# The input projection of a gated ConvFFN by seven products of quarter blocks in place of eight

## The chip, the cores and the metric

The kernel runs on one core of one Trainium2 chip, in one launch. The metric is the device time of a run in microseconds (us), lower is better. The engines are named as the profile names them: PE is TensorE's matmul and PEld its weight load, DVE is VectorE, ACT is ScalarE, POOL is GpSimd, SP is SyncE, whose queue issues nearly all transfers.

## The reference

A trunk of two layers works on 1024 tokens of 1024 features in float32. Each layer adds three branches to the residual stream x: token mixing by four groups of heads, cross-attention to 256 memory tokens, and a gated feed-forward network with a convolution over three tokens. The last one is what matters here:

```python
def conv_ffn(xn, w_in, conv_w, conv_b, w_out):
    h = xn @ w_in
    gate, up = h[..., :D_FF], h[..., D_FF:]
    gp = jnp.pad(gate, ((0, 0), (1, 1), (0, 0)))
    gconv = gp[:, :-2] * conv_w[0] + gp[:, 1:-1] * conv_w[1] + gp[:, 2:] * conv_w[2] + conv_b
    return (jax.nn.silu(gconv) * up) @ w_out

x = x + conv_ffn(rms_norm(x, norm_ffn[l]), w_ffn_in[l], ffn_conv[l], ffn_conv_b[l], w_ffn_out[l])
```

D_FF is 2816, so `w_in` is 1024 x 5632 and `w_out` 2816 x 1024.

## The kernel before

**Layout.** Features lie on partitions and tokens along the free axis: a tile is [128, 1024], 128 features of all tokens. x is 8 such tiles and lives in DRAM (`XD`). A matmul multiplies a block of weights [128 features in, 128 features out] with a tile's tokens, 512 columns at a time, one PSUM bank each.

**Pairs.** Every operand of a large product is split into `hi` (a cast to float32r, on ScalarE) and `lo` (the remainder, a subtraction on VectorE). A product takes three passes, hi hi, hi lo and lo hi (`dense_steps`, lines 344 to 348). `weights` (line 309) loads a block of 512 KB into a "raw" buffer (two of them) and makes its pair in the buffers "whi" and "wlo" (two of each).

**Pools.** Tag "h" has 16 tiles of [128, 1024], tag "t" 16 (work tiles), tag "z" 4 (side tiles), tag "s" 6 small tiles of 512 columns; PSUM has "sc" (two of two banks), "tp" (three banks) and "fl" (one).

**The ffn.** `run` (line 1551) ends the cross-attention with a residual product: `residual` (line 1253) goes over the eight output tiles m, loads x, multiplies, adds from PSUM (line 1260), stores x, and calls `done`. Here that is `finish_x` (line 369): it makes the pair of x times the norm's gain, and adds its squares to the sum in `RB` by ScalarE and GpSimd (line 235). `stats_end` (line 237) turns the sums into the norm's factor per token, spread over partitions in `RB`, with small matmuls (lines 245 and 254). So the ffn's inputs H are 8 pairs in 16 "h" tiles, not yet scaled by the norm's factor; that is put on the products.

The 22 tiles of inner features are made by `ffn_tile` (line 1524), eight, eight and six of them, and after each group the residual product over the group's pairs follows (eight tiles m, weights `w_ffn_out`). A tile multiplies H with the gate's weights and with up's weights: 2 blocks x 8 k x 3 passes x 2 token halves. VectorE takes the gate from PSUM with the norm's factor (line 1531), ScalarE and VectorE make the convolution (lines 1532 to 1539), ScalarE Silu (line 1540), VectorE takes up (line 1543), GpSimd multiplies (line 1544), and the pair of the output goes to two "t" tiles (lines 1546 and 1547).

**Order.** Each engine works through its own queue in order. The order in each queue is set when the kernel is built, by a scheduler that goes by priority (program order) and a timeline; a tile's buffer is reused when the last reader of its former owner is done, and buffers of one tag are handed out in program order. SP's queue holds the transfers of all of these in one line.

Of the kernel before, what the change touches and what calls it, by code (L numbers as in the profile page):

```python
# [30 lines left out]
# columns of the per-layer parameter block  # L31
# [8 lines left out]
# columns of the constants  # L40
# [3 lines left out]
# bands of 128 columns that spread compact rows over partitions  # L44
# [4 lines left out]
class Net:  # L49
# [69 lines left out]
    # --------------------------------------- work that runs in between other work  # L119
    def fill(self, gen, which=0):  # L120
        """Queues a generator that yields the time of what it has emitted."""
        self.queues[which].append(gen)
        return gen

    def pump(self, us, which=0):
        """Emits queued work of about us."""
# [23 lines left out]
    # ---------------------------------------------------------------- set-up  # L150
    def setup(self):
# [37 lines left out]
        self.OD = self.dram([KT, P, S], F32, "od")  # L189

# [3 lines left out]
    # -------------------------------------------------------- reciprocal roots  # L194
    def rsqrt(self, v, out, n):
        """out = 1 / sqrt(v) on [128, n]: bits halved, a Newton step, a step of third order."""
# [17 lines left out]
    # ------------------------------------------------------------ model norms  # L214
    def split_scaled(self, x, g, hi, lo, lo_engine=None):
        """hi + lo = x * g, each of them exact in float32r."""
# [9 lines left out]
    def stats_add(self, st, x, sq=None):  # L226
        """Adds x * x of one tile of features."""
# [9 lines left out]
    def stats_end(self, st, RB, bank=None):  # L237
        """r token-major [128, n / 128], spread over partitions into RB [128, n], and 1 / r^2."""
# [22 lines left out]
    # --------------------------------------------- norms over groups of features  # L261
    def group_sums(self, ps, G, g0, sq, ind, nt=8):
        """Sums of squares per token (partitions) and group: ps[:, t, g0:...]."""
# [7 lines left out]
    def group_rsqrt(self, ps, G, dim, inv, nt=8, times=1.0):  # L271
        """[128, nt * G] of times * r / sqrt(r^2 * mean + eps), of a stream that r still has to scale; inv = 1 / r^2."""
# [14 lines left out]
    def group_spread(self, y, G, band, banks, use, nt=8, rows=None):  # L287
        """Spreads the groups over partitions: use(slice, PSUM) for each half of the tokens.

        Rows over tokens as a float32r pair, g and 32 + g, which a band of ones adds up."""  # L290
# [17 lines left out]
    # ------------------------------------------------------------ dense layers  # L308
    def weights(self, src, K=KT, M=P, lo_engine=None, pool=None):
        """A [128, K, M] block of weights as a float32r pair."""  # L310
# [1341 lines left out]
def _tiles(w):  # L1652
    """[K, 128 n] as n blocks [128, K / 128, 128]."""
    k, n = w.shape
    return w.reshape(k // P, P, n // P, P).transpose(2, 1, 0, 3)
# [79 lines left out]
```

## Time and profile before

| | |
|---|---|
| median of three runs | 3649.74 us (3646.77 to 3653.95) |
| the profiled execution | span of 3645.1 us, 43780 instructions |
| granted TensorE clock, mean | 0.950 |
| busy: PE, DVE, ACT, POOL | 93%, 48%, 35%, 25% of the span |
| ffn of layer 0, with the last residual of cross-attention behind it | about 1117 to 1831 us |
| ffn of layer 1 | about 2930 to 3645 us |

The profile is of one execution. Busy time is the time in which an engine executes; the duration of a matmul holds its way through the pipeline, so several overlap, and the distance from one start to the next is what it costs. Durations of VectorE and GpSimd hold what they wait for inside the instruction. "<-" behind an idle time names what ended it. L12 is line 12 of the kernel.

### The profile page before, as it was taken

What the parts mean: (1) busy time and instruction counts of PE and PEld (TensorE: products, weight loads), DVE (VectorE), ACT (ScalarE), POOL (GpSimd) and SP (SyncE); (2) the same over time, 40 slices, a digit from 0 to 9 for tenths busy, and PEclk for the clock granted to TensorE, in tenths of its full rate; (3) what the DMA queues carried; (4) which work ended last, traced back from release to release, by engine and by line L of the source; (5) the groups of instructions that cost most, each with busy time, mean ns of one, the idle gap of its engine ahead of it and who ended that gap; (6) DMA issues with size and microseconds to landing.
All of it is one profiled execution on the core that took longest, in us unless ns stands there. A gap on an engine that the chain in (4) does not pass through costs nothing. (4 is left out here: it accounts for less than half of the span.)

```text
span 3645.1 us, 43780 instructions
## 1 busy us (share of the span) xinstructions
PE 3407.1 (93%) x17372; PEld 2871.1 (79%) x17372; DVE 1749.7 (48%) x2588; ACT 1271.0 (35%) x2011; POOL 922.3 (25%) x577
## 2 busy tenths in 40 slices
PE   7899778999999999999998988789899999999999
PEld 7777567887778888888897767679777888888887
DVE  4554547875443423423436536669735344234232
ACT  4322446753432212212333225567535222122121
POOL 2221335752111101101113214357422111011010
PEclk9998689999999999999999987889999999999999
DMA  5333234413242131231343332354223411312313
GB/s 162 97 110 98 82 90 137 170 69 138 70 139 76 48 131 58 64 122 53 109 135 100 110 118 82 96 167 137 91 86 106 137 53 58 133 47 74 117 45 123
DMA packets 142624, 367.85 MB, mean 101 GB/s; under 512 B 29842, under 2 KB 46996, under 8 KB 142420
## 3 DMA queue, kind: packets, MB, share of 16 engines
q1 hardware_dynamic: 142196, 364.53, 30.8%
q8 instruction: 137, 2.24, 0.3%
q0 software_dynamic: 224, 0.52, 0.0%
q14 instruction: 67, 0.55, 0.0%
HBM read 252.81 MB, written 104.86 MB: 98 GB/s over the span
## 5 line engine op out<-in xcount | busy, mean ns | idle before, releaser
L319 ACT CAST whi<-raw 128x1024 fp32r<-128x1024 f32 (+2 forms) x262 | 258.4, 986 | 1156.2 <-PE sc L346 728.4
L348 PE MATMUL sc<-h,wlo 128*128 128x512 f32 x1568 | 504.1, 402 | 14.2 <-DVE wlo L320 14.2
L344 PE MATMUL sc<-h,whi 128*128 128x512 f32 x1568 | 504.1, 402 | 9.5 <-ACT h L714 5.3
L346 PE MATMUL sc<-h,whi 128*128 128x512 f32 x1568 | 502.0, 400 | 0.0
L1544 POOL TENSOR_TENSOR z<-z,z 128x1024 f32<-128x1024 f32 x44 | 143.2, 3254 | 1165.0 <-DVE z L1543 1015.2
L348 PEld LDWEIGHTS sc<-h,wlo 128*128 128x128 f32 x1568 | 301.8, 194 | 81.9 <-DVE wlo L320 16.3
L344 PEld LDWEIGHTS sc<-h,whi 128*128 128x128 f32 x1568 | 300.5, 194 | 77.9 <-ACT h L714 6.6
L346 PEld LDWEIGHTS sc<-h,whi 128*128 128x128 f32 x1568 | 301.8, 193 | 66.7 <-issue 2.7
L320 DVE TENSOR_TENSOR wlo<-raw,whi 128x1024 fp32r<-128x1024 f32 (+2 forms) x210 | 255.4, 1216 | 91.4 <-ACT whi L319 91.2
L1260 DVE TENSOR_TENSOR z<-sc,z 128x1024 f32<-128x1024 f32 x64 | 78.4, 1225 | 413.6 <-PE sc L348 413.6
L348 PE MATMUL sc<-t,wlo 128*128 128x512 f32 x896 | 276.4, 389 | 0.1
L346 PE MATMUL sc<-t,whi 128*128 128x512 f32 x896 | 276.2, 389 | 0.0
L344 PE MATMUL sc<-t,whi 128*128 128x512 f32 x896 | 275.7, 389 | 0.4 <-ACT whi L319 0.3
L467 DVE TENSOR_REDUCE smax<-sc 128x1 f32<-128x1024 f32 x192 | 233.6, 1217 | 75.6 <-PE sc L676 56.0
L470 ACT ACTIVATE h<-sc,smax 128x1024 f32<-128x1024 f32 x192 | 214.8, 1121 | 101.5 <-DVE smax L467 76.5
L530 DVE TENSOR_TENSOR s<-tp,s 128x512 fp32r<-128x512 f32 x256 | 173.1, 683 | 100.0 <-ACT s L529 98.2
L344 PE MATMUL fl<-h,whi 128*128 128x512 f32 (+1 forms) x480 | 177.0, 369 | 38.4 <-ACT z L1304 38.4
L348 PEld LDWEIGHTS sc<-t,wlo 128*128 128x128 f32 x896 | 168.0, 188 | 35.8 <-DVE wlo L320 1.0
L344 PEld LDWEIGHTS sc<-t,whi 128*128 128x128 f32 x896 | 168.0, 188 | 35.6 <-ACT whi L319 0.9
L235 POOL TENSOR_TENSOR rb<-rb,z 128x1024 f32<-128x1024 f32 x42 | 114.0, 2713 | 324.2 <-ACT z L234 315.9
L346 PEld LDWEIGHTS sc<-t,whi 128*128 128x128 f32 x896 | 168.2, 188 | 34.9
L525 PE MATMUL tp<-identr,h 128*128 128x128 f32 x1024 | 178.8, 281 | 12.0 <-DVE s L530 8.1
(378 smaller groups left out, 6905.8 us busy)
## 6 DMA issues: line engine op xcount, KB each, us to landing
raw<-w_ffn_in SPq DMA_DIRECT2D x88, 512.0 KB
xd<-z SPq DMA_DIRECT2D x72, 512.0 KB
z<-xd SPq DMA_DIRECT2D x72, 512.0 KB
raw<-w_ffn_out SPq DMA_DIRECT2D x32, 512.0 KB
raw<-w_fm SPq DMA_DIRECT2D x30, 512.0 KB
z<-xT SPq DMA_DIRECT2D x16, 512.0 KB
raw<-w_ck SPq DMA_DIRECT2D x16, 512.0 KB
raw<-w_cv SPq DMA_DIRECT2D x16, 512.0 KB
```

What stands on the lines that cost most here:

```text
L235: nc.gpsimd.tensor_tensor(out=st["acc"], in0=st["acc"], in1=sq, op=ALU.add)
L319: nc.scalar.copy(hi, raw)
L320: (lo_engine or nc.vector).tensor_tensor(out=lo, in0=raw, in1=hi.bitcast(F32), op=ALU.subtract)
L344: nc.tensor.matmul(o, lhsT=hi[:, k, :], rhs=xh[:, f : f + m], start=first, stop=False)
L346: nc.tensor.matmul(o, lhsT=hi[:, k, :], rhs=xl[:, f : f + m], start=False, stop=False)
L348: nc.tensor.matmul(o, lhsT=lo[:, k, :], rhs=xh[:, f : f + m], start=False, stop=last)
L467: nc.vector.tensor_reduce(out=m, in_=sc, axis=AX.X, op=ALU.max, negate=True)
L470: nc.scalar.activation(e, sc, AF.Exp, bias=m, scale=1.0, accum_out=s)
L525: nc.tensor.transpose(tp[:, (2 * j + i) * P : (2 * j + i + 1) * P], w[:, (k + j) * P : (k + j + 1) * P], self.ident)
L530: nc.vector.tensor_tensor(out=el, in0=tp, in1=eh.bitcast(F32), op=ALU.subtract)
L1260: nc.vector.tensor_tensor(out=x, in0=ps, in1=x, op=ALU.add)
L1544: nc.gpsimd.tensor_tensor(out=c, in0=c, in1=g, op=ALU.mult)
```

## The change

The product [gate; up] = W^T H of one tile is seen as a product of 2 x 2 blocks: gate and up are the two rows of blocks, the two halves of the 1024 input features are the inner blocks, the two halves of the tokens are the columns. The form of Winograd and Strassen makes it of seven products of quarter blocks (`PRODUCTS`), each over 4 k and 512 tokens, with sums ahead of and behind them.

- The sums of token blocks are made once in a layer. `ffn_operands` takes the place of `finish_x`: x times the gain is kept whole, and for each of the four k, tile m = k and tile m = k + 4 give seven operands (`quarter_sums`, four sums, two on each of VectorE and GpSimd), each as a pair in one [128, 1024] tile. The residual goes over m in the order 0, 4, 1, 5, 2, 6, 3, 7. For m = 3 and 7 x is scaled in place. 28 tiles of "h" and "t" hold them.
- The sums of weight blocks are made in every tile, four on GpSimd from the two raw blocks, and seven pairs of half size go to the buffers "whi" and "wlo" in turn.
- Products follow one another in three PSUM banks X, Z and Y; X gathers four of them and is read in between; gate and up are put together in SBUF by three copies and three additions, then scaled by `RB`.
- The tile's output goes to DRAM (`GD`). All 22 tiles are made first. Then the three residual products follow, whose operands `load_pair` reads back through a side tile.

Everything else is the same; comments and docstrings are removed.

```diff
         self.OD = self.dram([KT, P, S], F32, "od")
+        self.GD = self.dram([FT, P, S], F32, "gd")
...
-    def residual(self, wsrc, K, H, xsrc, xdst, done=None, alloc=None):
-        nc = self.nc
-        for m in range(KT):
+    def residual(self, wsrc, K, H, xsrc, xdst, done=None, alloc=None, order=range(KT)):
+        nc = self.nc
+        for m in order:
             x = (alloc or self.z_)()
             nc.sync.dma_start(out=x, in_=xsrc[m])
             ps = self.dense_full(self.weights(wsrc(m), K=K), H)
...
-    def ffn_tile(self, l, f, H, alloc):
+    def half_pair(self, x, g, b, lo_engine=None):
+        nc = self.nc
+        hi, lo = b[:, :HF], b[:, HF:]
+        if g is None:
+            nc.scalar.copy(hi, x)
+            (lo_engine or nc.vector).tensor_tensor(out=lo, in0=x, in1=hi.bitcast(F32), op=ALU.subtract)
+        else:
+            self.split_scaled(x, g, hi, lo)
+        return hi, lo
+    def quarter_sums(self, a, b):
+        nc = self.nc
+        tt = nc.gpsimd.tensor_tensor
+        a1, a2, b1, b2 = a[:, :HF], a[:, HF:], b[:, :HF], b[:, HF:]
+        t1, t2, t3, t4 = (self.s_() for _ in range(4))
+        nc.vector.tensor_tensor(out=t1, in0=a2, in1=a1, op=ALU.subtract)
+        nc.vector.tensor_tensor(out=t3, in0=b2, in1=a2, op=ALU.subtract)
+        tt(out=t2, in0=b2, in1=t1, op=ALU.subtract)
+        tt(out=t4, in0=b1, in1=t2, op=ALU.subtract)
+        return {"11": a1, "21": b1, "t2": t2, "t1": t1, "t3": t3, "22": b2, "t4": t4}
+    def ffn_operands(self, l, B):
+        nc = self.nc
+        seen, late = {}, []
+        st = self.stats_begin()
+        def done(m, x):
+            k = m % 4
+            self.stats_add(st, x, self.t_() if k == 3 else None)
+            y = x if k == 3 else self.t_()
+            nc.scalar.activation(y, x, AF.Identity, bias=0.0, scale=self.col(l, C_FFN + m))
+            seen[m] = y
+            if m < 4:
+                return
+            a, b = seen.pop(k), seen.pop(m)
+            if k < 2:
+                for n, v in self.quarter_sums(a, b).items():
+                    B[n].append(self.half_pair(v, None, (self.tr_ if n == "11" else self.h_)()))
+            else:
+                late.append((a, b))
+        def end():
+            sums = [self.quarter_sums(a, b) for a, b in late[:1]]
+            for n in self.PRODUCTS:
+                for i in range(2):
+                    if i == len(sums):
+                        sums.append(self.quarter_sums(*late[1]))
+                    B[n].append(self.half_pair(sums[i][n], None, (self.h_ if n in ("22", "t4") else self.tr_)()))
+        return st, done, end
+    PRODUCTS = ("11", "21", "t2", "t1", "t3", "22", "t4")
+    def ffn_in_tile(self, l, f, B, dst):
         nc, d = self.nc, self.d
-        gp = self.sc_()
-        self.dense(self.weights(d["w_ffn_in"][l, f, 0]), H, [gp[:, :HF], gp[:, HF:]])
-        up = [self.fl_(), self.pv_()]
-        self.dense(self.weights(d["w_ffn_in"][l, f, 1]), H, up)
-        g, c = self.z_(), self.z_()
-        nc.vector.tensor_tensor(out=g, in0=gp, in1=self.RB, op=ALU.mult)
+        raw = []
+        for i in range(2):
+            r = self.tile(self.pw, [P, S], F32, "raw", bufs=2)
+            nc.sync.dma_start(out=r.rearrange("p (k m) -> p k m", m=P), in_=d["w_ffn_in"][l, f, i])
+            raw.append(r)
+        a11, a12, a21, a22 = (r[:, h * HF : (h + 1) * HF] for r in raw for h in range(2))
+        s1, s2, s3, s4 = (self.s_() for _ in range(4))
+        tt = nc.gpsimd.tensor_tensor
+        tt(out=s1, in0=a21, in1=a22, op=ALU.add)
+        tt(out=s2, in0=s1, in1=a11, op=ALU.subtract)
+        tt(out=s3, in0=a11, in1=a21, op=ALU.subtract)
+        tt(out=s4, in0=a12, in1=s2, op=ALU.subtract)
+        A = {"11": a11, "21": a12, "t2": s2, "t1": s1, "t3": s3, "22": s4, "t4": a22}
+        pair = {}
+        for i, n in enumerate(self.PRODUCTS):
+            pair[n] = self.half_pair(A[n], None, self.tile(self.pw, [P, S], F32R, ("whi", "wlo")[i % 2], bufs=2))
+        xz = self.sc_()
+        X, Z, Y = xz[:, :HF], xz[:, HF:], self.pv_()
+        def product(n, ps, first):
+            hi, lo = (t.rearrange("p (k m) -> p k m", m=P) for t in pair[n])
+            for k, (bh, bl) in enumerate(B[n]):
+                mm = lambda a, b, start, stop: nc.tensor.matmul(
+                    ps, lhsT=a, rhs=b, start=start, stop=stop, skip_group_check=not first
+                )
+                mm(hi[:, k], bh, first and k == 0, False)
+                mm(hi[:, k], bl, False, False)
+                mm(lo[:, k], bh, False, k == 3)
+        g, u, c = self.z_(), self.t_(), self.z_()
+        g1, g2, u1, u2 = g[:, :HF], g[:, HF:], u[:, :HF], u[:, HF:]
+        add = lambda o, ps: nc.vector.tensor_tensor(out=o, in0=ps, in1=o, op=ALU.add)
+        product("11", X, True)
+        nc.scalar.copy(g1, X)
+        product("21", Z, True)
+        add(g1, Z)
+        product("t2", X, False)
+        nc.scalar.copy(g2, X)
+        product("t1", Y, True)
+        nc.scalar.copy(u2, Y)
+        product("t3", X, False)
+        add(u2, X)
+        product("22", Y, False)
+        add(g2, Y)
+        product("t4", X, False)
+        nc.vector.tensor_tensor(out=g, in0=g, in1=self.RB, op=ALU.mult)
+        nc.vector.tensor_tensor(out=u2, in0=u2, in1=self.RB[:, HF:], op=ALU.mult)
         nc.scalar.activation(c, g, AF.Identity, bias=self.col(l, C_CB + f), scale=self.col(l, C_W1 + f))
         nc.vector.scalar_tensor_tensor(
             out=c[:, 1:], in0=g[:, : S - 1], scalar=self.col(l, C_W0 + f), in1=c[:, 1:], op0=ALU.mult, op1=ALU.add
@@ -1538,16 +1645,11 @@
             op0=ALU.mult, op1=ALU.add,
         )
         nc.scalar.activation(c, c, AF.Silu)
-        for n, p in enumerate(up):
-            sl = slice(n * HF, (n + 1) * HF)
-            nc.vector.tensor_tensor(out=g[:, sl], in0=p, in1=self.RB[:, sl], op=ALU.mult)
-        nc.gpsimd.tensor_tensor(out=c, in0=c, in1=g, op=ALU.mult)
-        hi, lo = alloc(F32R), alloc(F32R)
-        nc.scalar.copy(hi, c)
-        nc.vector.tensor_tensor(out=lo, in0=c, in1=hi.bitcast(F32), op=ALU.subtract)
-        return hi, lo
+        nc.vector.tensor_tensor(out=u1, in0=X, in1=self.RB[:, :HF], op=ALU.mult)
+        nc.gpsimd.tensor_tensor(out=u, in0=c, in1=u, op=ALU.mult)
+        nc.sync.dma_start(out=dst, in_=u)
...
-            st, H = self.stats_begin(), []
+            B = {n: [] for n in self.PRODUCTS}
+            st, done, end = self.ffn_operands(l, B)
             self.residual(
-                lambda m: d["w_co"][l, m], KT, O, self.XD, self.XD,
-                lambda m, x: H.append(self.finish_x(l, C_FFN, m, x, st, self.h_)),
+                lambda m: d["w_co"][l, m], KT, O, self.XD, self.XD, done, order=(0, 4, 1, 5, 2, 6, 3, 7)
             )
             self.stats_end(st, self.RB)
+            end()
+            for f in range(FT):
+                self.ffn_in_tile(l, f, B, self.GD[f])
             last = l == DEPTH - 1
             st, Hn = self.stats_begin(), []
-            for f0, n in ((0, 8), (8, 8), (16, 6)):
-                G = [self.ffn_tile(l, f0 + i, H, self.tr_) for i in range(n)]
+            for f0, n, alloc in ((0, 8, self.tr_), (8, 8, self.h_), (16, 6, self.tr_)):
+                G = [self.load_pair(self.GD[f0 + i], alloc) for i in range(n)]
```

## Rows read from the trace of the kernel before

**Rows 1.** The page, busy time of the engines (share of the span).

```profile
span 3645.1 us, 43780 instructions
...
PE 3407.1 (93%) x17372; PEld 2871.1 (79%) x17372; DVE 1749.7 (48%) x2588; ACT 1271.0 (35%) x2011; POOL 922.3 (25%) x577
```

**Rows 2.** Table by stage: length, busy (x count) per engine, clock, DMA, GB/s.

```profile
500.00:1040.00 540.00, 491.52 (x3048) 427.21 (x3049) 364.79 (x623) 302.38 (x558) 239.51 (x169) 0.96 0.34 115
...
1117.00:1831.00 714.00, 714.00 (x3168) 591.78 (x3167) 255.50 (x243) 161.10 (x152) 86.57 (x28) 1.00 0.26 83
...
2930.00:3645.00 715.00, 709.97 (x3145) 588.18 (x3144) 242.22 (x233) 143.08 (x134) 71.60 (x22) 1.00 0.25 81
```

**Rows 3.** Timelines of VectorE and ScalarE, one ffn tile: start, length, instruction, idle before.

```profile
1239.12 1.23 DVE L1531 TENSOR_TENSOR z<-sc,rb 128x1024 f32<-128x1024 f32 x1 [4.08 <-PE sc L348]
1240.26 1.22 DVE L320 TENSOR_TENSOR wlo<-raw,whi 128x1024 fp32r<-128x1024 f32 x1
1241.65 1.28 DVE L1533 SCALAR_TENSOR_TENSOR z<-z,par,z 128x1023 f32<-128x1023 f32 x1 [0.18 <-ACT z L1532]
1242.98 1.29 DVE L1536 SCALAR_TENSOR_TENSOR z<-z,par,z 128x1023 f32<-128x1023 f32 x1
...
1250.38 0.68 DVE L1543 TENSOR_TENSOR z<-tp,rb 128x512 f32<-128x512 f32 x1
1250.97 1.22 DVE L320 TENSOR_TENSOR wlo<-raw,whi 128x1024 fp32r<-128x1024 f32 x1
...
1260.87 1.23 DVE L1531 TENSOR_TENSOR z<-sc,rb 128x1024 f32<-128x1024 f32 x1 [4.09 <-PE sc L348]
...
1240.38 1.25 ACT L1532 ACTIVATE z<-z,par 128x1024 f32<-128x1024 f32 x1 [0.66 <-DVE z L1531]
1244.36 1.06 ACT L1540 ACTIVATE z<-z 128x1024 f32<-128x1024 f32 x1 [2.73 <-DVE z L1536]
```

**Rows 4.** Timeline of TensorE, six matmuls into one bank in cross-attention.

```profile
2772.74 0.39 PE L1464 MATMUL tp<-s,z 128*128 128x512 f32 x1
...
2773.89 0.40 PE L1466 MATMUL tp<-s,z 128*128 128x512 f32 x1
```

**Rows 5.** Groups by line and shape: count, busy us, mean ns, idle before.

```profile
L319 ACT CAST whi<-raw 128x1024 fp32r<-128x1024 f32 x214 | 225.3, 1053 | 1050.6 <-PE sc L346 662.0 <-PE tp L346 156.4 <-issue 154.0
...
L530 DVE TENSOR_TENSOR s<-tp,s 128x512 fp32r<-128x512 f32 x256 | 173.1, 683 | 100.0 <-ACT s L529 98.2 <-PE fl L346 0.8
L499 POOL TENSOR_TENSOR h<-h,h 128x1024 f32<-128x1024 f32 x64 | 153.9, 2405 | 2.2
L529 ACT CAST s<-tp 128x512 fp32r<-128x512 f32 x256 | 149.1, 589 | 92.7 <-PE tp L525 90.3
...
L1445 POOL TENSOR_TENSOR e<-e,csum 128x512 f32<-128x512 f32 x16 | 18.3, 1161 | 26.8 <-DVE csum L1442 17.5 <-PE fl L299 8.6 <-PE tp L1453 0.8
```

**Rows 6.** Timelines of GpSimd and VectorE where both work in SBUF at once.

```profile
774.52 2.38 POOL L499 TENSOR_TENSOR h<-h,h 128x1024 f32<-128x1024 f32 x1
...
774.96 2.49 DVE L715 TENSOR_TENSOR h<-h,h 128x512 fp32r<-128x512 f32 x1
...
1251.23 3.22 POOL L1544 TENSOR_TENSOR z<-z,z 128x1024 f32<-128x1024 f32 x1 [18.53 <-DVE z L1543]
```

**Rows 7.** Chain of waits at 2823 us (a load), then SP's queue at 1306 us.

```profile
2823.09 3.62 DMA raw<-w_co
...
1306.33 0.32 SPq L1261 DMA_DIRECT2D xd<-z  x1
...
1309.10 0.32 SPq L1258 DMA_DIRECT2D z<-xd  x1
```

**Rows 8.** VectorE in the residual ahead of the ffn; chain of waits, the norm's matmuls.

```profile
1094.03 1.23 DVE L1260 TENSOR_TENSOR z<-sc,z 128x1024 f32<-128x1024 f32 x1 [7.15 <-PE sc L348]
...
1104.91 1.23 DVE L1260 TENSOR_TENSOR z<-sc,z 128x1024 f32<-128x1024 f32 x1 [7.15 <-PE sc L348]
...
2929.35 1.68 PE fl L245 x16
...
2938.17 0.89 PE fl L254 x8
```

## Prediction, written before the change was run

> **What bounds the kernel now.** I read the page's busy times first. TensorE is busy for 93% of the span and VectorE, the next, for 48% [rows 1], but that is a mean over stages, so the second view is the table by stage. In it the reader is to see that the two stretches of the ffn are of another kind than the rest: TensorE is busy in 714.00 of 714.00 us and in 709.97 of 715.00 us, at a granted clock of 1.00, which is the level of 2.4 GHz, while VectorE is busy for 36% of the first stretch, ScalarE for 23%, GpSimd for 12%, and the DMA engines take a quarter of their time [rows 2]. So in the stage that is changed the matmuls set the end, and every matmul less there is time less until another engine or a wait takes over.
>
> The third view is the timeline of VectorE over one ffn tile. The gate product of one tile is taken from PSUM at 1239.12 and that of the next at 1260.87, 21.75 us later [rows 3]. In between lie 2 weight blocks x 8 k x 3 passes x 2 halves = 96 matmuls, 0.2266 us each. The eight residual products around the ffn show the same: 10.88 us from one evacuation to the next for 48 matmuls [rows 8].
>
> **What is removed.** The seven products take 7 x 4 k x 3 passes = 84 matmuls of 512 columns per tile in place of 96. There are 22 tiles in each of 2 layers, so 12 x 44 = 528 matmuls go. At 0.2267 us that is 119.7 us, or 2.72 us per tile; the new tile is 84 x 0.2267 = 19.04 us of TensorE. One product is 12 matmuls = 2.72 us, and since exactly one is saved, a tile that makes TensorE wait for 2.72 us gains nothing.
>
> The twelve matmuls of a product all accumulate into one bank, where before two banks took turns. The nearest row is the value product of the cross-attention, six matmuls of 512 columns into one bank: they start from 2772.74 to 2773.89, five steps in 1.15 us, 0.230 us each [rows 4]. Against 0.2267 that would cost 0.003 x 84 x 44 = 12 us; the ffn's own rows say nothing. I take a third, 4 us.
>
> **What is added in a tile, engine by engine.** VectorE before: two weight remainders (1.22 each), the gate's scaling (1.23), two convolution steps (1.28 and 1.29), two halves of up (0.68 each) and the output's remainder (1.23, the row of its like), 8.8 us. After: seven remainders of half size, three additions from PSUM, a scaling of 1024 and two of 512 columns, and the same two convolution steps: 7 x 0.68 + 3 x 0.68 + 1.22 + 2 x 0.68 + 2.57 = 12.0 us [rows 3, 5]. ScalarE: seven casts and three copies of 512 columns at 0.59, and the convolution's pass and Silu at 1.25 and 1.06, 8.2 us [rows 3, 5]. GpSimd: four sums of 512 columns at 1.16 and the product with Silu at 2.41, 7.0 us [rows 5]. Each is below 19.04 us, so TensorE stays first if these were free of each other.
>
> They are not. GpSimd's 2.38 us operation of 774.52 ends at 776.90; VectorE's subtraction of 512 columns that started at 774.96 takes 2.49 us in place of 0.68, until 777.45, so it ran after the other had ended. The reverse is there too: the GpSimd product of 1251.23 takes 3.22 us in place of 2.41 behind the remainder that VectorE began at 1250.97 [rows 3, 6]. VectorE's operations with one source in PSUM do not show it: their mean over 256 is 0.68 us [rows 5], in stages where GpSimd works for 44% of the time [rows 2]. So remainders, scalings of what is already in SBUF and convolution steps exclude GpSimd's sums. If the two engines never overlapped at all, a tile would need 12.0 + 7.0 = 19.0 us of the pair, as much as TensorE; at the time for 512 columns that a straight half of 2.41 would give no more than 0.2 is added. The cost is thus between nothing and what waits inside that chain add (rival 1: up to 64 us in all). The lead of the buffers decides. A weight pair gets its buffer two to four products ahead of its use (two tags of two buffers, seven pairs), at least 5.4 us for a cast and a remainder of 1.27 us; a bank that is written again has one other product in between, 2.72 us for a copy of 0.59 or an addition of 0.68. A remainder that is held up by a GpSimd sum (1.16) still fits into both. Only behind the product with Silu (2.41) would an addition be late, by 2.41 + 0.68 + 0.68 - 2.72 = 1.05 us, and that product falls early in the next tile, where no addition has a near due time. I take 0.2 us per tile, 9 us.
>
> The Trainium skill (SBUF — State Buffer, section "SBUF: two separate sides") speaks against this change: it says that a VectorE operation with two sources in SBUF and a GpSimd operation that reads SBUF hold one pair of ports for the whole instruction, and that the later one is blocked. The trace agrees, by the 2.49 us above. Taken for all operations of a tile it gives the serial 19.0 to 19.2 us, the floor of the first rival; with engines free of each other the 9 us would be nothing.
>
> **The weights' chain.** Both raw blocks of a tile fill the two raw buffers. The second comes free when the last pair ("t4") is made, which waits for the third product: 8.16 us into the tile, plus 1.3. Then a load (3.62 us from issue to landing as the chain of waits has it [rows 7]), two sums (2.3), the pair (1.3): 16.7 us; the pair is needed in the next tile's third product at 19.04 + 5.44 = 24.5. About 8 us are left, and GpSimd's product (2.4) or waits for VectorE fit in. Nothing.
>
> **DRAM instead of SBUF.** 22 stores and 22 loads of 512 KB in each layer are added; the stage moves 83 GB/s with 26% of the DMA engines' time [rows 2], and one store per tile adds 27 GB/s. SP's queue issues them; a store waits there for the product with Silu, and what stands behind it is the second raw load with its 8 us. The cast and remainder of each output move from the tile to `load_pair`, in the residual, where VectorE has 1.22 + 1.23 us of work in each 10.88. The later groups' loads hide there, through the four side tiles.
>
> **The seams.** Before the first tile, the last quarter sums need the residual tile of m = 7. It is now scaled in place, so after the addition (1.23) its store must have read it: a side tile is reloaded 2.77 us after the issue of its store [rows 7]. Then the scaled copy (1.25), a cast (0.59) and a remainder (0.68): 6.5 us. Covered are product "11", which needs only m = 3, and three quarters of "21": 21 matmuls, 4.8 us. Left: 1.7 us, into which the norm's matmuls (1.68 and twice 0.89 [rows 8]) may fall; with semaphores and sums I take 3 us. Bounds: 0, and 10 if the sums queue up on GpSimd behind the squares' addition.
>
> After the last tile, the first residual needs eight pairs from DRAM. The pool of 16 work tiles holds seven and a half of them until u of tile 21 has been stored: 0.68 + 1.22 + 1.25 + 2.57 + 1.06 + 2.41 + 2.77 = 12.0 us from the end of product "22", 9.2 after the last matmul, plus a remainder of 1.22. TensorE reaches that half after 44 matmuls, 10.0 us. The loads before it go through two free side tiles at about 5.9 us each (3.62 + 1.05 + 1.22), four or five before the tile's end. I take 3 us; bounds 0 and 10. Both seams, both layers: 12 us.
>
> **Sum.** 3645.1 - 119.7 + 4 + 9 + 12 = 3550.4 us of span. The page gives the profiled execution by its span; the median of the three runs, 3649.74, is 4.6 above it. Predicted: 3555 us, own range 3535 to 3565.
>
> **Rivals.** (1) The port pair becomes the bound. For it: 19.0 us against 19.04. Against it: additions from PSUM and all of ScalarE run beside. With 0.5 to 1.5 us of waits between dependent steps (before, VectorE stands 0.18 us before a convolution step [rows 3]) a tile is 19.5 to 20.5 us in place of 19.2, which is 11 to 55 us more: 3566 to 3610. (2) The seams take 10 us each: 28 more, 3583. (3) Slower: the additions and copies that free a bank come late in every tile. TensorE waits at four places (before "t2", "t3", "22", "t4"); if ScalarE's and VectorE's queues put a cast or a remainder that itself waits ahead of each, each costs its lateness. From 0.68 us at each of four places the saving is gone; at 1.3 each, 5.2 per tile, it is 3555 + 44 x 5.0 = 3775. Against it: before, a cast follows TensorE's release at once, and VectorE stood idle for 4.09 us before 1260.87 [rows 3]. (4) The waits come to just the saving: 3643 to 3657.
>
> **Chances.** Forecast 0.58; rival 1 0.24; rival 2 0.07; between these and before 0.02; no change 0.03; slower 0.06. A measurement of this kernel can tell 0.2% from no change. Faster 0.91, same 0.03, slower 0.06. The range 3532 to 3612 begins at the saving without any wait (3530) and takes in rivals 1 and 2; it leaves out about 0.12.
>
> **What would show it.** Right: TensorE without gaps inside the stage, a tile period of 19.0 to 19.3 us, 16844 matmuls, and idle time of a few us at the two seams alone. Rival 1: a period above 19.5 with VectorE remainders and GpSimd sums stretched, TensorE released by remainders. Rival 3: TensorE released by copies and additions before "t2", "t3", "22", "t4". The prediction is wrong if the order on the engines' queues makes waits that the durations do not ask for.

## The result and the profile after

The changed kernel takes 3804.18 us (median of four runs, 3796.07 to 3810.86) against 3648.26 for the kernel before beside it: a ratio of 1.0431, 95% interval 1.0399 to 1.0464. It is slower by 4.3%, where 3555 us, 2.6% faster, was forecast. The page of the profiled execution, with the matmuls and the busy times:

```profile
span 3794.3 us, 44182 instructions
...
PE 3360.4 (89%) x16844; PEld 2770.9 (73%) x16844; DVE 2238.8 (59%) x2996; ACT 1451.3 (38%) x2419; POOL 1252.6 (33%) x769
```

The 528 matmuls are gone, as forecast, and yet the span is 149.2 us longer than in [rows 1]. The table by stage says where to look. The columns are those of [rows 2]; the first row is the start of the ffn of layer 0, the second its steady tiles:

```profile
1123.50:1143.50 20.00, 15.32 (x45) 12.51 (x46) 16.83 (x30) 8.27 (x15) 10.33 (x6) 0.59 0.08 27
1165.60:1662.00 496.40, 414.22 (x1716) 315.62 (x1716) 359.40 (x307) 160.01 (x244) 207.61 (x101) 1.00 0.20 66
```

Before, TensorE had no idle time in this stage [rows 2]; now it stands for 82 of 496 us, with no other engine near full. Such a picture (the bounding engine with gaps, nothing else saturated) means waits, so the next view is TensorE's timeline, here for one tile period, from a "t3" to the next; a bracket gives the idle time and what ended it:

```profile
1197.90 1.65 PE L1614 MATMUL sc<-h,whi 128*128 128x512 f32 x6 [1.19 <-ACT z L1629]
1199.39 1.52 PE L1614 MATMUL sc<-t,whi 128*128 128x512 f32 x6
1201.70 3.03 PE L1614 MATMUL sc<-h,whi 128*128 128x512 f32 x12 [0.78 <-DVE t L1623]
1204.57 0.61 PE L1614 MATMUL sc<-t,whi 128*128 128x512 f32 x2
1205.02 0.61 PE L1614 MATMUL tp<-h,wlo 128*128 128x512 f32 x2
1206.30 2.56 PE L1614 MATMUL sc<-t,whi 128*128 128x512 f32 x10 [0.66 <-DVE whi L1540]
1210.22 1.20 PE L1614 MATMUL tp<-h,wlo 128*128 128x512 f32 x4 [1.36 <-DVE wlo L1540]
...
1215.34 2.88 PE L1614 MATMUL tp<-h,wlo 128*128 128x512 f32 x12
1218.06 1.52 PE L1614 MATMUL sc<-h,whi 128*128 128x512 f32 x6
...
1222.14 1.65 PE L1614 MATMUL sc<-h,whi 128*128 128x512 f32 x6 [1.19 <-ACT z L1629]
```

A period is 24.24 us (1197.90 to 1222.14), 5.2 more than 84 matmuls need. Twelve matmuls into one bank take 2.72 us from start to start (1215.34 to 1218.06), so their rate is that of before. What is new is the order. The program calls 11, 21, t2, t1, t3, 22, t4. TensorE's queue holds two matmuls of "11" and of "t1" of the coming tile first, then the rest of both, 21, 22, and last t2, t3 and t4 side by side. Those three go into the same bank X, and "t3" and "t4" wait until X has been read: 1.19 us for a copy, 0.78 for an addition. The rest of "11" and of "t1" wait for remainders (0.66 and 1.36). The brackets hold 3.99 of the 5.2 us; from start to start each of these gaps is 0.2 to 0.3 longer, and behind three of them the first step costs some 0.1 more. The table of waits has the four over the whole kernel:

```profile
PE tp L1614 <- DVE wlo L1540: 57.0, 44, 5.0
PE sc L1614 <- ACT z L1629: 50.1, 42, 1.2
...
PE sc L1614 <- DVE whi L1540: 33.4, 40, 1.7
PE sc L1614 <- DVE t L1623: 32.9, 42, 0.8
```

Why the remainders are late is in the timelines of VectorE, ScalarE, GpSimd and SP's queue around them:

```profile
1196.75 0.62 ACT L1539 CAST whi<-raw 128x512 fp32r<-128x512 f32 x1 [4.82 <-PE sc L1614]
1197.27 0.58 ACT L1629 COPY z<-sc 128x512 f32<-128x512 f32 x1
1197.40 0.69 DVE L1540 TENSOR_TENSOR whi<-raw,whi 128x512 fp32r<-128x512 f32 x1 [4.74 <-ACT whi L1539]
...
1198.12 11.85 SPq L1595 DMA_DIRECT2D raw<-w_ffn_in  x2
...
1201.72 2.27 POOL L1600 TENSOR_TENSOR s<-raw 128x512 f32<-128x512 f32 x1 [12.35 <-DMA raw<-w_ffn_in]
1202.76 1.78 DVE L1638 TENSOR_TENSOR t<-t,rb 128x512 f32<-128x512 f32 x1
1204.07 1.62 POOL L1601 TENSOR_TENSOR s<-s,raw 128x512 f32<-128x512 f32 x1
1204.46 1.78 DVE L1540 TENSOR_TENSOR whi<-raw,whi 128x512 fp32r<-128x512 f32 x1
1205.66 1.73 POOL L1602 TENSOR_TENSOR s<-raw,raw 128x512 f32<-128x512 f32 x1
...
1208.40 1.77 DVE L1540 TENSOR_TENSOR wlo<-s,wlo 128x512 fp32r<-128x512 f32 x1
```

VectorE and GpSimd take turns, and 0.69 us becomes 1.8. They meet there because GpSimd's sums wait for the raw load. It is issued 0.03 us after the remainder of "t4" has ended (1197.40 and 0.69), the last reader of its buffer; and that pair gets a buffer of its own only when "t2" is done, which stands near the end of the queue. ScalarE's cast for that pair also stands ahead of the copy that "t3" waits for: both are released by the end of "t2", and the copy starts 0.52 us behind the cast.

Last, the start of layer 0's ffn on TensorE:

```profile
1117.89 1.52 PE L1614 MATMUL sc<-t,whi 128*128 128x512 f32 x6
1121.03 0.50 PE L1614 MATMUL sc<-t,whi 128*128 128x512 f32 x1 [1.61 <-ACT t L1539]
1123.57 2.50 PE L1614 MATMUL sc<-t,whi 128*128 128x512 f32 x5 [2.04 <-DVE t L1540]
1125.87 3.41 PE L246 MATMUL fl<-cons,rb 128*128 128x1 f32 x16
1129.13 2.91 PE L1614 MATMUL sc<-h,wlo 128*128 128x512 f32 x6
1131.84 2.21 PE L1614 MATMUL sc<-t,wlo 128*128 128x512 f32 x6
...
1139.13 2.07 PE L1614 MATMUL tp<-h,wlo 128*128 128x512 f32 x4 [4.62 <-DVE wlo L1540]
...
1153.59 0.62 PE L1614 MATMUL tp<-h,wlo 128*128 128x512 f32 x2
...
1159.80 2.88 PE L1614 MATMUL sc<-t,whi 128*128 128x512 f32 x12
```

Six matmuls run, then TensorE waits for 1.61 and 2.04 us, and the next six matmuls take 2.71 us from start to start (1129.13 to 1131.84) in place of 1.36, as at the lower level of 1.2 GHz. A third wait, of 4.62 us, follows; the granted clock of the whole stretch is 0.59 (first row of the table by stage). The "11" of the second tile begins 41.9 us after that of the first (1117.89 to 1159.80). "t1" of the second tile is done by then (from 1153.59), so 96 matmuls lie in between, which need 21.8 us: some 20 us are lost.

### The profile page after: what moved, and what is told of

Same layout as the page of the kernel before. It is cut to its first block, busy times and chain, and to the rows that moved or that the text cites. A ratio compares the mean times of both kernels' runs of the same rounds, so it can differ in the third digit from the quotient of the medians.

```text
span 3794.3 us, 44182 instructions
## 1 busy us (share of the span) xinstructions
PE 3360.4 (89%) x16844; PEld 2770.9 (73%) x16844; DVE 2238.8 (59%) x2996; ACT 1451.3 (38%) x2419; POOL 1252.6 (33%) x769
## 5 line engine op out<-in xcount | busy, mean ns | idle before, releaser
L320 ACT CAST whi<-raw 128x1024 fp32r<-128x1024 f32 (+2 forms) x174 | 165.3, 950 | 623.7 <-PE sc L347 437.2
L349 PE MATMUL sc<-h,wlo 128*128 128x512 f32 x1120 | 366.6, 408 | 13.2 <-DVE wlo L321 13.2
L1614 PE MATMUL sc<-h,whi 128*128 128x512 f32 x1056 | 273.2, 400 | 84.6 <-ACT z L1629 50.1
L1614 PE MATMUL sc<-t,whi 128*128 128x512 f32 x1056 | 275.5, 396 | 40.7 <-DVE whi L1540 33.4
L1614 PEld LDWEIGHTS sc<-h,whi 128*128 128x128 f32 x1056 | 191.7, 188 | 158.7 <-ACT z L1629 67.9
L1614 PEld LDWEIGHTS sc<-t,whi 128*128 128x128 f32 x1056 | 195.6, 188 | 98.5 <-DVE whi L1540 50.3
L349 PEld LDWEIGHTS sc<-h,wlo 128*128 128x128 f32 x1120 | 217.9, 197 | 63.9 <-DVE wlo L321 15.3
L1614 PE MATMUL tp<-h,wlo 128*128 128x512 f32 x792 | 209.4, 400 | 58.6 <-DVE wlo L1540 57.0
L345 PEld LDWEIGHTS sc<-h,whi 128*128 128x128 f32 x1120 | 217.2, 197 | 60.5 <-ACT h L715 6.6
L1600 POOL TENSOR_TENSOR s<-raw 128x512 f32<-128x512 f32 x44 | 88.5, 2011 | 520.3 <-DMA raw<-w_ffn_in 518.9
L347 PEld LDWEIGHTS sc<-h,whi 128*128 128x128 f32 x1120 | 218.1, 196 | 51.1 <-issue 3.9
L1614 PEld LDWEIGHTS tp<-h,wlo 128*128 128x128 f32 x792 | 146.1, 189 | 106.1 <-DVE wlo L1540 75.8
L1540 DVE TENSOR_TENSOR whi<-raw,whi 128x512 fp32r<-128x512 f32 x88 | 104.1, 1183 | 201.6 <-ACT whi L1539 201.6
L347 PE MATMUL sc<-t,whi 128*128 128x512 f32 x640 | 197.4, 389 | 3.5 <-DVE t L1230 3.5
L345 PE MATMUL sc<-t,whi 128*128 128x512 f32 x640 | 196.7, 390 | 3.3 <-ACT t L1229 2.6
```

Source lines behind the costliest of these rows:

```text
L320: nc.scalar.copy(hi, raw)
L345: nc.tensor.matmul(o, lhsT=hi[:, k, :], rhs=xh[:, f : f + m], start=first, stop=False)
L347: nc.tensor.matmul(o, lhsT=hi[:, k, :], rhs=xl[:, f : f + m], start=False, stop=False)
L349: nc.tensor.matmul(o, lhsT=lo[:, k, :], rhs=xh[:, f : f + m], start=False, stop=last)
L1540: (lo_engine or nc.vector).tensor_tensor(out=lo, in0=x, in1=hi.bitcast(F32), op=ALU.subtract)
L1600: tt(out=s1, in0=a21, in1=a22, op=ALU.add)
```

## The experiments

A tile's period is given as the mean distance between GpSimd's products with Silu, from the third to the last tile of layer 0; for the changed kernel it is 24.09 us. All ratios are to the kernel before.

**Order alone.** The products are held in the program's order on TensorE.

```diff
+            behind = self.tc.issue_after(self.last.ins) if self.last else nullcontext()
+            with behind:
                 for k, (bh, bl) in enumerate(B[n]):
...
+                    self.last = mm(lo[:, k], bh, False, k == 3)
```

> The seven-product kernel with one thing added: every product's matmuls are queued behind the last matmul of the product before it, so TensorE's queue has the order of the program text (11, 21, t2, t1, t3, 22, t4). Theory A (the order in TensorE's queue made the waits): both kinds of wait go, since each reading of bank X has another product beside it and the sums are due later; a tile takes 19.0 to 19.8 us in place of 24.2, the median is 3570 to 3620 us. Theory B (the exclusion of VectorE and GpSimd made them, the order only shows where): the 2.6 us for the bank go, the 2.6 us for remainders stay; 21.6 us per tile, 3680 to 3700 us.

Measured: 3726.78 us, 1.0230 (1.0209 to 1.0251); period 22.47. Better by 77 us, but neither number is met. In TensorE's timeline the waits for remainders are gone from the steady tiles, and two others are there:

```profile
1250.62 1.66 PE L1616 MATMUL sc<-h,wlo 128*128 128x512 f32 x6 [1.75 <-ACT z L1627]
...
1254.49 1.66 PE L1616 MATMUL sc<-h,whi 128*128 128x512 f32 x6 [0.85 <-DVE z L1625]
```

The first is "21" (its weights are in "wlo"), which writes Z and waits for the copy of X. The second is "t2", which writes X and waits for the addition from Z. Neither needs the other's bank. But X and Z are the two halves of one tile "sc", and that is what the framework's semaphores go by.

**Sums on VectorE, order free.**

```diff
-        tt = nc.gpsimd.tensor_tensor
+        tt = nc.vector.tensor_tensor
```

> The seven-product kernel with the four sums of weight blocks on VectorE in place of GpSimd, order left to the scheduler. Theory A: the waits for bank X (2.6 us per tile) stay as long as t2, t3 and t4 stand next to each other in TensorE's queue; 21.5 us per tile or more, 3680 to 3720 us. Theory B: nothing but the product with Silu is left on GpSimd, the remainders come in time; 19.5 to 20.5 us per tile, 3590 to 3640 us.

Measured: 3678.48 us, 1.0093 (1.0076 to 1.0110); period 21.68: Theory A, just under its range. The waits for copy and addition stay to the tenth (50.1 and 32.9 us); those for the remainders shrink from 90.4 to 6.4. In this order the place of the sums is worth 126 us. How much of it is the alternation, and how much that one sum takes VectorE less time than GpSimd (0.69 against 1.16 us [rows 5]), is not separated.

**Both.**

> Both edits: products queued in the order of the text, sums of weight blocks on VectorE. Theory A: within 20 us of the run with the order alone, since nothing waits for GpSimd there; 3570 to 3620 us. Theory B: about 100 us below the run with the order alone.

Measured: 3691.18 us, 1.0130 (1.0113 to 1.0147); period 21.77. That is neither theory: 36 us under the run with the order alone. "21" still waits for the copy of X (52.4 us in all) and "t2" for the addition from Z (40.6). With the sums off GpSimd the order alone is worth nothing (3691 against 3678); the waits between X and Z are the next limit.

**The trip through DRAM alone.** The kernel before, whose 22 outputs go to DRAM and come back through `load_pair`, as in the change.

```diff
+            for f in range(FT):
+                self.ffn_tile(l, f, H, self.GD[f])
+            for f0, n, alloc in ((0, 8, self.tr_), (8, 8, self.h_), (16, 6, self.tr_)):
+                G = [self.load_pair(self.GD[f0 + i], alloc) for i in range(n)]
```

> The kernel before with one part of the change alone: eight products as before, but all 22 outputs go to DRAM and come back as pairs ahead of the three residual products. If the round trip costs only the seam behind the last tile, as the forecast had it: 3 to 6 us per layer, 3655 to 3662 us. Rival: the stage's transfers or the side tiles delay the residual products too: 3675 us or more.

Measured: 3664.64 us, 1.0054 (1.0036 to 1.0071). That lies between the two expectations. The trip costs 20 us by the ratio; the profiled execution (span 3646.2, 1.1 over before) was the shortest of six and shows no new wait, so its place is not shown. It is no large part of the loss.

**Separate tiles.** X, Z and Y in tiles of their own, order free, sums on GpSimd.

```diff
-        xz = self.sc_()
-        X, Z, Y = xz[:, :HF], xz[:, HF:], self.pv_()
+        X, Z, Y = self.sc_()[:, :HF], self.fl_(), self.pv_()
```

> The changed kernel with X, Z and Y in three separate PSUM tiles in place of X and Z as the two halves of one; the order is left to the scheduler, the sums s1 to s4 stay on GpSimd. Theory A (the two halves of one tile are tied: a product into one waits for the reader of the other, and this is also what makes the scheduler pull t1 ahead and leaves t2, t3 and t4 side by side): the waits before the products for the copy of g and the addition of u2, 50.1 and 32.9 us in all, go; the weights' waits for the VectorE remainders, 57.0 and 33.4 us, stay or shrink: a tile of 21.6 us or less, 3650 to 3720. Theory B (the waits are the latency of copies and additions themselves, whatever the tile): within 15 us of the changed kernel, 3790 to 3820.

Measured: 3670.74 us, 1.0067 (1.0045 to 1.0088); period 21.15. Theory A. The waits for copy and addition, 50.1 and 32.9 us, are no longer among those of 3.2 us or more. TensorE's queue now begins a tile with "21", and the rest of the loss is weights (ScalarE's casts 43.0, VectorE's remainders 26.7).

**The same with the sums on VectorE.**

> Separate PSUM tiles for X, Z and Y as in the run before it, and the sums s1 to s4 on VectorE in place of GpSimd; the order is left to the scheduler. Theory A: with the tie between the halves and the alternation of VectorE and GpSimd both gone, a tile comes near its 84 matmuls, 19.04 us, at most 19.8; about 2.0 to 2.7 us a tile under the kernel before, 88 to 119 us over 44 tiles, against some 40 us lost in the two seams of each layer: 3560 to 3610, faster than the kernel before. Theory B: no better than the changed kernel with its sums on VectorE, 3665 to 3690.

Measured: 3702.01 us, 1.0150 (1.0127 to 1.0172); period 22.01. Missed: the better place for the sums makes it worse. The scheduler's order is another one again; TensorE waits for ScalarE's casts (42.9) and for the addition of u2 (41.2). With a free order an edit is measured together with whatever order it brings.

**Separate tiles, pinned order, sums on VectorE.**

> Separate PSUM tiles, sums on VectorE, and the products held in the order of the program on TensorE. Theory A: the 1.25 us before product 21 (for the copy of X) and the 0.85 us before t2 (for the addition from Z), which stood in the pinned order with X and Z in one tile, are gone, a tile of 19.0 to 19.8 us, 3560 to 3610 as for the free order: once the tie is cut, the order is worth under 15 us. Theory B: the waits before 21 and t2 stay, 3680 to 3700.

Measured: 3651.71 us, 1.0018 (1.0007 to 1.0029); period 20.11. The waits before "21" and "t2" are gone, as Theory A has it, but not its time. Two waits were hidden behind them: 41.3 us for the addition before "t4", and 20.2 us in the first tiles, where "21" must stand behind the statistics, since Z is now in their only bank "fl".

**Three runs on these two waits.** First Z from the rotating banks:

```diff
-        X, Z, Y = self.sc_()[:, :HF], self.fl_(), self.pv_()
+        X, Z, Y = self.sc_()[:, :HF], self.pv_(), self.pv_()
```

> As the run with separate tiles, pinned order and sums on VectorE, and Z taken from the three banks that Y rotates through, in place of the one bank that the statistics of the seam use too. Theory A (the 10.1 us and 0.7 us before the statistics' transposes, and the clock at half while TensorE waits there, come from the product 21 of the first tile, which in pinned order must wait for the statistics' bank): tile 0 of each layer shrinks by 10 us or more, 3615 to 3635. Theory B (the seam is bound by the y and sum chain before the first tile, whatever the bank): within 8 us of 3652. The 1.0 us before t4 stays under both.

Measured: 3625.95 us, 0.9948 (0.9932 to 0.9964): 26 us better, Theory A. What is left before "t4" is read on VectorE's queue:

```profile
1228.14 0.69 DVE L1600 TENSOR_TENSOR s<-raw 128x512 f32<-128x512 f32 x1 [1.80 <-DMA raw<-w_ffn_in]
1228.87 0.69 DVE L1601 TENSOR_TENSOR s<-s,raw 128x512 f32<-128x512 f32 x1
1229.48 0.69 DVE L1602 TENSOR_TENSOR s<-raw,raw 128x512 f32<-128x512 f32 x1
1230.08 0.68 DVE L1624 TENSOR_TENSOR t<-sc,t 128x512 f32<-128x512 f32 x1
1230.82 3.01 PE L1615 MATMUL sc<-h,whi 128*128 128x512 f32 x12 [0.91 <-DVE t L1624]
```

Three sums of the next tile's weights, of which the first waits for its load, stand in front of the addition that frees X. Sums back on GpSimd, all else as in this run:

> As the run before it in this list (Z from the rotating banks, separate tiles, pinned order), with the sums s1 to s4 back on GpSimd. Theory A (VectorE and GpSimd alternate on SBUF operands, and the late remainders are what that costs): the wait before t4 for the addition goes, since no sum stands before it on VectorE any more, but it or the remainders come late by the alternation: 1 to 3 us a tile over 19.04, so 3600 to 3690. Theory B (the alternation is harmless once the order is fixed): a tile at 19.1 us, 3570 to 3595.

Measured: 3581.85 us, 0.9828 (0.9810 to 0.9847); period 19.01. And on VectorE, but behind the addition of the tile before:

```diff
+        with self.tc.issue_after(self.added.ins) if self.added else nullcontext():
+            tt(out=s1, in0=a21, in1=a22, op=ALU.add)
...
-        add(u2, X)
+        self.added = add(u2, X)
```

> As the first of this list, with the sums s1 to s4 on VectorE held behind the addition of u2 of the tile before. Theory A (t4 waits some 1.0 us a tile because on VectorE the sums, which wait for the load of the raw weights, stand in front of the addition that frees bank X): the wait before t4, 41.3 us in all, goes; a tile of 19.0 to 19.2 us; 35 to 45 us under the first of this list, so 3570 to 3600, faster than the kernel before. Theory B (the addition is late for its own sake, a semaphore and 0.69 us behind t3): within 10 us of the first of this list.

Measured: 3580.82 us, 0.9825 (0.9806 to 0.9844); period 19.11. Theory A: the wait before "t4" was the sums' place in the queue. The two are equal, and both beat the kernel before by 1.7%: the one with the sums on GpSimd, called the mended change below, differs from the changed kernel only in the pinned order of the products and in the tiles of X and Z. Its table by stage, then VectorE and GpSimd in it:

```profile
1165.60:1560.00 394.40, 394.23 (x1736) 325.17 (x1735) 318.81 (x308) 161.86 (x249) 187.58 (x101) 1.00 0.24 83
```

```profile
1237.25 1.74 POOL L1602 TENSOR_TENSOR s<-raw,raw 128x512 f32<-128x512 f32 x1
1238.95 1.74 POOL L1603 TENSOR_TENSOR s<-raw,s 128x512 f32<-128x512 f32 x1
...
1239.46 2.31 DVE L1638 TENSOR_TENSOR z<-z,rb 128x1024 f32<-128x1024 f32 x1
```

TensorE is busy in 394.23 of 394.40 us although the two engines still hold each other up (1.22 us becomes 2.31). Theory A of that run, that they must cost 1 to 3 us a tile, is refuted.

**The missing corner.** Z from the rotating banks as in the mended change, order free.

> The changed kernel with X, Z and Y in three separate tiles, Z from the rotating banks, in the scheduler's free order, sums on GpSimd: only the tiles are changed. Theory A (the tie between the halves is what makes the scheduler's order bad; cut, any order runs without a stall): 3582 to 3600, as in the pinned order. Theory B (order and tiles each carry a part: the free order still calls t1 and 21 before 11, whose remainders come late behind GpSimd's sums): 3630 to 3680, near the 3671 of the run with Z in the statistics' bank.

Measured: 3694.06 us, 1.0142 (1.0125 to 1.0159); period 21.89. Theory B. It stands even over its range and over the 3670.74 of the run with Z in "fl": another order, in which t2, t3 and t4 follow each other in every second tile. With sums on GpSimd the four corners are:

| median, us | X and Z halves of one tile | separate tiles |
|---|---|---|
| order free | 3804 | 3694 |
| order of the program | 3727 | 3582 |

Order alone is worth 77 us, tiles alone 110, both 222.

**The start of the ffn.** Here the mended change still loses 19.9 us a layer: its first tile takes 38.98 us on TensorE, from the first "11" to the second (1123.80 to 1162.78, below), where 84 matmuls need 19.04. The 40.8, 41.7 and 22 us in the expectations below run on to the second "21" and so hold twelve matmuls, 2.72 us, of the second tile. First, in the run with the sums behind the addition, the activation sums on VectorE too:

```diff
     def quarter_sums(self, a, b):
-        tt = nc.gpsimd.tensor_tensor
+        tt = nc.vector.tensor_tensor
```

> As the run with the sums of the weights behind the addition, and the two sums per pair of activation tiles that stood on GpSimd (t2 and t4 of the quarter sums) on VectorE too, so that GpSimd has little left in the seam before the first tile. Theory A (the first tile takes 40.8 us in place of 19 because VectorE and GpSimd alternate while the last activation sums and their remainders are made): the remainders take 0.69 us in place of 1.2 to 2.5 and the waits before the first t2 product, 4.21 and 1.82 us, shrink by 3 us or more a layer: 3568 to 3576. Theory B (the number of VectorE's operations behind the last activation tile sets it, whichever engine makes two of them): within 5 us of 3581.

Measured: 3583.59 us, 0.9843 (0.9826 to 0.9861). Theory B: taking these sums off GpSimd gains nothing. Then fewer small buffers at a time:

```diff
-        t1, t2, t3, t4 = (self.s_() for _ in range(4))
+        t1, t2, t4, t3 = *(self.s_() for _ in range(3)), a2
...
-        s1, s2, s3, s4 = (self.s_() for _ in range(4))
+        s1, s2, s4, s3 = *(self.s_() for _ in range(3)), a21
```

> As the run before it, and t3 of the activation sums and s3 of the weight sums are written over a quarter that nothing reads any more, so that three of the six small buffers are taken at a time in place of four. Theory C (the sums of the first tile's weights stand late because the small buffers are still held by the activation sums): the sums s1 to s4 of tile 0 come before the last activation sums, and the first tile is 4 us or more shorter than in the run before it, 3560 to 3573. If buffers don't bind, within 5 us of the run before it.

Measured: 3584.81 us, 0.9842 (0.9823 to 0.9860). Theory C falls. Last, the pair of activation tiles that comes last is not summed and split; the operands of the third pair stand in its place:

```diff
-                for i in range(2):
-                    if i == len(sums):
-                        sums.append(self.quarter_sums(*late[1]))
-                    B[n].append(self.half_pair(sums[i][n], ...))
+                B[n].append(self.half_pair(sums[0][n], ...))
+                B[n].append(B[n][-1])
```

> The kernel with separate tiles, pinned order and sums on GpSimd, in which the last of the four pairs of activation tiles (3 and 7) is not summed and split: each product's fourth quarter takes the operands of the third again. This leaves out six sums, seven casts and seven remainders a layer, and the wait for the last output tile of w_co; the matmuls stay 84 a tile, the statistics and the scaling stay. Theory A (the first tile's 22 us over 19 are the chain behind the last pair: its sums, its 14 splits and, at half the granted clock, the products that wait on them): the first tile takes 22 to 28 us in place of 41.7, so 3545 to 3560. Theory B (the statistics, their square root and the transposes on the one bank hold the first tile): within 8 us of 3582.

Measured: 0.9798 (0.9772 to 0.9823); three runs of 3564.54 to 3580.45 us; a fourth, of 9438.62, is left out of the ratio. Between the two theories. The first tile of layer 0 on TensorE, in the mended change:

```profile
1123.80 1.52 PE L1615 MATMUL sc<-t,whi 128*128 128x512 f32 x6
1126.93 0.50 PE L1615 MATMUL sc<-t,whi 128*128 128x512 f32 x1 [1.61 <-ACT t L1539]
1129.46 2.37 PE L1615 MATMUL sc<-t,whi 128*128 128x512 f32 x5 [2.04 <-DVE t L1540]
...
1140.76 1.22 PE L1615 MATMUL sc<-h,whi 128*128 128x512 f32 x2 [3.77 <-ACT whi L1539]
1145.44 2.07 PE L1615 MATMUL sc<-h,whi 128*128 128x512 f32 x4 [3.46 <-DVE whi L1540]
...
1162.78 2.88 PE L1615 MATMUL sc<-t,whi 128*128 128x512 f32 x12
```

and without the last pair:

```profile
1118.73 1.52 PE L1613 MATMUL sc<-t,whi 128*128 128x512 f32 x6
1121.85 0.49 PE L1613 MATMUL sc<-t,whi 128*128 128x512 f32 x1 [1.60 <-ACT t L1539]
1124.42 2.50 PE L1613 MATMUL sc<-t,whi 128*128 128x512 f32 x5 [2.08 <-DVE t L1540]
...
1148.29 2.88 PE L1613 MATMUL sc<-t,whi 128*128 128x512 f32 x12
```

The later two waits, 7.2 us, go with the last pair; the first two stay. The first tile takes 29.6 us (1118.73 to 1148.29) in place of 39.0: 9.4 a layer, 18.8 in all, and the spans differ by 18.3. So the 19.9 us are 9.4 for the last pair and, in the run without it, 3.7 of waits for the pair before, 3.3 of the norm's small matmuls (which the kernel before has too), 2.7 for 17 matmuls below full clock (0.57 from 1123 to 1131 us), and 0.8 in small gaps.

## Why the prediction was wrong, point by point

- **Matmuls saved, 119.7 us.** Right: 16844 matmuls, 2.72 us a product, and a period of 19.01 to 19.11 us where nothing waits, against 19.04. The 4 us for one bank came to nothing.
- **The failed step** is "a bank that is written again has one other product in between, 2.72 us". It took TensorE's order from the program, though a scheduler sets each queue. In the queue that was built, t2, t3 and t4 follow one another, and each of the two waits costs its reader's whole time (0.78 us for an addition of 0.69; 1.19 for a copy of 0.58 that also stands behind a cast). The same order leaves the remainders no lead, the other half of the loss (0.66 and 1.36 us a tile): with the order pinned these waits are gone from the steady tiles. The prediction's own sign of being wrong was such an order. Held in the program's order the step is still false, by a second mistake of the same step: it counts banks, where the dependency goes by tiles, and X and Z are one tile. Both are shown by the four corners above: neither mend alone comes under the kernel before. The Trainium skill (Perfetto Trace Analysis, section "Matmuls") says to rotate independent products through different banks, so that the evacuation of one runs beside the next. The trace agrees: 1.19 and 0.78 us where products into X stand side by side, none in the steady tiles of the mended change, where they alternate with products into banks of other tiles.
- **The port pair, 0.2 us a tile.** Right in the order that the step assumed, and even too much: 19.01 us with GpSimd's sums, 19.11 without. In the order that was built, where the remainders have no lead, the sums on GpSimd made 2.4 us of the tile's 5.05 (24.09 against 21.68), and moving them gained 126 us. The Trainium skill (SBUF — State Buffer, section "SBUF: two separate sides") calls the ports that VectorE and GpSimd share an exclusive lock, held for a whole instruction. The trace agrees in both kernels: 1.78 us for 0.69 in the changed one, 2.31 for 1.22 in the mended one. Whether it costs time was decided here by the lead of the remainders.
- **The weights' chain, "about 8 us are left".** Right for the assumed order (no wait for a load in the mended change), gone in the built one, where "t4" frees the raw buffer last.
- **DRAM.** Taken as nothing, measured at 20 us in the kernel before (13 to 26 by the interval's ends). The account below needs no such term in the mended change beside the end of the ffn, so what it costs there is open.
- **The start of the ffn, 3 us a layer.** Mis-sized: 19.9 in the mended change, 16.6 of them new. The step counted 21 matmuls of cover. Only six ran, because the third pair's splits, too, are made behind the last residual tile (`late` holds both); and it left out the clock. **The end of the ffn, 3 us a layer:** right in the changed kernel, 1.76 and 1.34 us of waits; in the mended one 6.6, of which 3.5 are a wait for the first pair from DRAM and some 3 the matmuls behind it, at a granted clock of 0.66 from 1564 to 1574 us.
- **Rivals.** Number 3 is what happened, at 5.05 us a tile where it used 5.0, and 3775 against 3804; half of it by waits that it names (those before "t3" and "t4", 1.97 of the 3.99 us, though more for the order of the products than for queues ahead of the readers), half by late weights, which it doesn't name. It was given 0.06, on the ground that VectorE had had idle time before the change. But idle time says that an addition can run at once, not that its reader is far away in TensorE's queue.

The account per layer, from the last addition of w_co to the last of w_ffn_out on VectorE: 721.1 us before (1116.4 to 1837.5), 790.6 after (1118.2 to 1908.8), 686.0 in the mended change (1124.1 to 1810.1). After: 69.5 more, where 59.9 less was due: 129.4 lost, of which 21 periods of 5.05 over 19.04 are 106, and the start and end of the ffn are left with some 23. Mended: 35.1 less, 24.8 lost, of which 16.6 at the start (without the norm's matmuls, which are in both), 6.6 at the end and 1.3 in the 21 tiles between.

Why the scheduler put t1 ahead of 21 and left t2, t3 and t4 together was not found out. With the tie of X and Z cut it still left those three together in every second tile with Z in the rotating banks, and in none with Z in "fl".

## What to carry to other kernels

Where a scheduler writes the queues, cost a change by the order that will be built, not by the program: look for products into one bank that could come to stand side by side, and pin the order where the slack is of the size of what is saved. Give each PSUM bank that is read at its own time a tile of its own. And once a first wait is mended, look for the one behind it: here the partial mends stood between 2.3% slower and 0.5% faster than the kernel before, and the full one at 1.7% faster.

## What the runs showed that was not expected

- A product into one half of a two-bank tile waited for the reader of the other half: 1.75 us before "21", 0.85 before "t2", in nearly every tile (42 and 44 such waits in 44 tiles).
- With the same arithmetic, nothing but order, banks and the engine of four sums moved the time between 3581 and 3804 us.
- After waits of 1.61 and 2.04 us on TensorE, six matmuls took 2.71 us for 1.36; the granted clock of the 20 us from there, with one more wait of 4.62, was 0.59. In the steady tiles of the changed kernel, with 5.2 us of waits in each 24.2, it stayed at 1.00.
- VectorE and GpSimd held each other up in the mended change too (1.74 us for a sum of 1.16, 2.31 for a scaling of 1.22), with TensorE at 394.23 of 394.40 us busy.
